# A decoder trunk of four layers: output products with tokens on partitions and 512 weight columns at a time, and layer boundaries taken in two halves of the tokens

## The chip, the cores and the metric

The kernel runs on one core of one Trainium2 chip. The metric is device microseconds of one execution. All inputs lie in HBM when it starts, and the output is written back there. The engines are TensorE (PE in the profile; PEld is its loading of weights), VectorE (DVE), ScalarE (ACT), GpSimd (POOL) and SyncE (SP), which issues the large DMAs.

## What is computed

A residual stream `h` of 256 tokens by 1024 channels passes four layers. Each layer has a token mixer and a gated feed-forward with a convolution of width 3 along the tokens; around each of them stand two RMS norms:

```python
for i in range(4):
    a = rms_norm(h, mix_norm_pre[i])
    m = mixer(i % 3)(a)          # 0: dilated attention, 1: short gated convolution, 2: conformer convolution
    h = h + rms_norm(m, mix_norm_post[i])
    f = conv_ffn(rms_norm(h, ffn_norm_pre[i]), ffn_w_in[i], ffn_w_conv[i], ffn_w_out[i])
    h = h + rms_norm(f, ffn_norm_post[i])

def conv_ffn(x, w_in, w_conv, w_out):
    u = causal_dwconv(x @ w_in, w_conv)      # w_in: 1024 x 5632
    g, v = split(u, 2)
    return (silu(g) * v) @ w_out             # w_out: 2816 x 1024
```

The layers are attention, short convolution, conformer, attention. Everything is float32. The attention has 16 heads of 64 in each of three groups with dilations 1, 4 and 16; its tokens are put in an order in which those with equal remainder by 4 lie together ("permuted"). The conformer's output product has a bias.

## The kernel before, in words

**Precision.** A float32 product is made of three products of `float32r` parts: weights and inputs are each split into a high part and a rest (`mm3`, L278). So each weight tile is copied by ScalarE (L192) and subtracted by VectorE (L198) before use.

**Weights.** `plan` (L68) lists all weights in order of use in pieces of 128 x 1024; two pieces make a block of 1 MB, which SyncE loads (L182) into one of three raw buffers. `Stream` hands the parts out: 11 slots for split pieces (`SLOTS`), and calls of `pump`, `copy`, `diff` and `between`, written by hand among the other work, split the pieces ahead. `take` gives the next piece, and splits it on the spot if that has not been done. The whole kernel runs under a manual schedule: each engine runs its instructions in the order in which they are written.

**Layout.** Channels lie on partitions, tokens in the free dimension. The residual is eight tiles `h[k]` of 128 channels x 256 tokens. A product uses a 128 x 128 weight tile as the stationary operand and 256 tokens as the moving one: `column` (L461) makes one tile of 128 output columns with 8 x 3 products of 256 columns. `Slabs` (L509) accumulates the second product of the feed-forward and of the short convolution row slab by row slab: one piece is 128 rows by 1024 columns, 24 products of 256 columns (L521) in four PSUM banks, issued between the columns of the first product as their inputs come (`ffn_steps`, `sc_steps`); the last rows go by column tiles (`tail`). In the attention four output columns are accumulated while the last head pairs are worked off (L1012 to L1022); the conformer's output goes by columns.

**The boundary.** `Out` (L469) squares each finished column tile on ScalarE and scales it by the norm's gain; the sums of squares go through `rstd_of` (L299): products with a column of ones (L305), then six small operations. `spread` (L319) brings the token scale to all channels, `warm` (L327) issues products of no use. `boundary` (L340) then scales, adds into the residual, and makes the two parts of the next input, channel tile by channel tile. `start_norm` and `ramp` (L424) run four column tiles of the next product at once as these parts come. The scale of the next norm is found meanwhile and multiplied in when the products are read out (`evac`, L573, and its like). The last `boundary` (L386 to L393) writes the output in four DMAs.

**PSUM.** Tag A has four banks, B three, S one. The work tiles `act` have 32 buffers of 128 x 512.

## Time and profile before

| | us |
|---|---|
| median of 3 runs | 1616.36 |
| lowest to highest | 1616.09 to 1616.82 |
| span of the profiled execution, first to last instruction | 1615.5 |
| busy: TensorE | 1589.8 |
| busy: VectorE | 1243.3 |
| busy: ScalarE | 924.9 |
| busy: GpSimd | 18.5 |
| DMA | 256.94 MB, mean 159 GB/s |

The page gives the profiled execution by its span; it gives no other time for it, and the median stands 0.9 us above. TensorE's matmuls are pipelined: a record's length is longer than the distance to the next record, and the pace is read from the starts. A float32 matmul that is not `float32r` leaves two records.

### The profile page before, as it was taken

How to read it: one execution, taken by the hardware profiler on the slowest of the kernel's cores; microseconds unless marked ns; L12 is line 12 of the kernel's file. 1: busy time of each engine (PE TensorE's matmuls, PEld its weight loads, DVE VectorE, ACT ScalarE, POOL GpSimd, SP SyncE). 2: the span in 40 equal slices, each digit the busy share in tenths (PEclk: the TensorE clock that was granted, in tenths of full speed). 3: DMA queues.
4: the chain of work that ended last, by engine and by line, in shares of the span. 5: the costliest groups of instructions: out<-in, count | busy, mean ns of one | idle time of the engine just before them, and what ended most of it. 6: DMA issues, size and time to landing. Idle time of an engine off the chain costs nothing.

```text
span 1615.5 us, 31426 instructions
## 1 busy us (share of the span) xinstructions
PE 1589.8 (98%) x13146; PEld 1554.8 (96%) x13146; DVE 1243.3 (77%) x2177; ACT 924.9 (57%) x1623; POOL 18.5 (1%) x51
## 2 busy tenths in 40 slices
PE   6999999999999999999999999999999999999998
PEld 6999999999999999999999999999999999999998
DVE  4987767697876779889599588785877778588783
ACT  6454644575564566556476666565645445566562
POOL 4000000000000000000000000000000000000000
PEclk9999999999999999999999999999999999999999
DMA  5553442265552644655243136553543434236540
GB/s 213 214 213 121 170 144 105 90 235 199 183 185 95 216 157 160 232 183 191 97 150 112 53 127 230 192 183 132 186 180 133 155 131 157 105 131 227 191 157 27
DMA packets 36718, 256.94 MB, mean 159 GB/s; under 512 B 4320, under 2 KB 4448, under 8 KB 5984
## 3 DMA queue, kind: packets, MB, share of 16 engines
q1 hardware_dynamic: 36288, 254.93, 44.0%
q8 instruction: 103, 1.69, 0.4%
q14 instruction: 39, 0.32, 0.1%
q10 hardware_dynamic: 288, 0.01, 0.0%
HBM read 253.87 MB, written 1.05 MB: 158 GB/s over the span
## 4 chain that ended last, share of the span: by engine, by line
PE 95%; DVE 2%; POOL 1%; ACT 1%; DMA 1%; issue 0%; DVEq 0%; POOLq 0%
PE psA L521 17%; PE psB L281 10%; PE psB L280 10%; PE psB L279 10%; PE psA L279 8%; PE psA L280 7%; PE psA L281 7%; PE psA L877 3%; PE psA L879 3%; PE psA L878 3%; PE psB L714 2%; PE psB L896 2%; PE psB L925 2%; PE psA L437 2%; PE psA L432 2%; PE psB L914 2%
## 5 line engine op out<-in xcount | busy, mean ns | idle before, releaser
L198 DVE TENSOR_TENSOR wlo<-raw,whi 128x1024 fp32r<-128x1024 f32 x480 | 579.9, 1220 | 41.8 <-ACT whi L192 40.6
L192 ACT CAST whi<-raw 128x1024 fp32r<-128x1024 f32 x480 | 490.0, 1046 | 22.2 <-DMA raw<-in_w_dram 16.6
L281 PE MATMUL psB<-act,wlo 128*128 128x256 f32 x1392 | 394.2, 283 | 0.0
L280 PE MATMUL psB<-act,whi 128*128 128x256 f32 x1392 | 394.2, 283 | 0.0
L279 PE MATMUL psB<-act,whi 128*128 128x256 f32 x1392 | 394.2, 283 | 0.0
L279 PE MATMUL psA<-act,whi 128*128 128x256 f32 x1040 | 303.6, 292 | 8.0 <-ACT whi L192 7.1
L281 PE MATMUL psA<-act,wlo 128*128 128x256 f32 x1040 | 295.2, 284 | 0.5 <-DVE wlo L198 0.5
L280 PE MATMUL psA<-act,whi 128*128 128x256 f32 x1040 | 295.3, 284 | 0.1
L521 PE MATMUL psA<-act,whi 128*128 128x256 f32 x1536 | 278.0, 283 | 0.0
L279 PEld LDWEIGHTS psB<-act,whi 128*128 128x128 f32 x1392 | 267.4, 192 | 0.0
L281 PEld LDWEIGHTS psB<-act,wlo 128*128 128x128 f32 x1392 | 267.4, 192 | 0.0
L280 PEld LDWEIGHTS psB<-act,whi 128*128 128x128 f32 x1392 | 267.4, 192 | 0.0
L521 PEld LDWEIGHTS psA<-act,whi 128*128 128x128 f32 x1536 | 239.7, 192 | 0.0
L521 PE MATMUL psA<-act,wlo 128*128 128x256 f32 x768 | 217.5, 283 | 0.0
L279 PEld LDWEIGHTS psA<-act,whi 128*128 128x128 f32 x1040 | 200.0, 192 | 12.8 <-ACT whi L192 7.1
L281 PEld LDWEIGHTS psA<-act,wlo 128*128 128x128 f32 x1040 | 200.1, 192 | 0.8 <-DVE wlo L198 0.8
L280 PEld LDWEIGHTS psA<-act,whi 128*128 128x128 f32 x1040 | 200.2, 192 | 0.6 <-DVE act L284 0.5
L290 ACT ACTIVATE tmp<-act,par 128x256 f32<-128x256 f32 x176 | 80.1, 502 | 176.6 <-DVE act L284 176.6
L287 DVE SCALAR_TENSOR_TENSOR tmp<-act,par,tmp 128x255 f32<-128x255 f32 (+1 forms) x352 | 146.6, 478 | 19.7 <-ACT tmp L290 19.7
L521 PEld LDWEIGHTS psA<-act,wlo 128*128 128x128 f32 x768 | 147.5, 192 | 0.0
L284 DVE TENSOR_TENSOR act<-psB,act 128x512 f32<-128x512 f32 (+2 forms) x94 | 58.4, 624 | 101.5 <-PE psB L281 60.1
L877 PE MATMUL psA<-whi,act 128*128 128x256 f32 x384 | 112.4, 293 | 0.0
(124 smaller groups left out, 2129.7 us busy)
## 6 DMA issues: line engine op xcount, KB each, us to landing
raw<-in_w_dram SPq DMA_DIRECT2D x239, 1024.0 KB, 4.8
h<-in_xT_dram SPq DMA_DIRECT2D x4, 256.0 KB, 5.1
raw<-in_w_dram SPq DMA_DIRECT2D x2, 512.0 KB, 5.5
out_dram<-h SPq DMA_DIRECT2D x4, 256.0 KB, 2.1
msk<-in_masks_dram SPq DMA_DIRECT2D x1, 512.0 KB, 9.4
par<-in_params_dram SPq DMA_DIRECT2D x1, 484.0 KB, 10.1
cst<-in_consts_dram SPq DMA_DIRECT2D x1, 132.0 KB, 5.9
par<-in_params_dram ACTq DMA_DIRECT2D x1, 4.0 KB, 2.9
```

The source lines that it names most:

```text
L192: self.nc.scalar.copy(out=hi, in_=raw)
L198: self.nc.vector.tensor_tensor(out=lo, in0=raw, in1=hi.bitcast(F32), op=ALU.subtract)
L279: nc.tensor.matmul(o, lhsT=whi, rhs=x[0], start=first, stop=False)
L280: nc.tensor.matmul(o, lhsT=whi, rhs=x[1], start=False, stop=False)
L281: nc.tensor.matmul(o, lhsT=wlo, rhs=x[0], start=False, stop=last)
L284: nc.vector.tensor_tensor(out=out, in0=a, in1=b, op=op)
L287: nc.vector.scalar_tensor_tensor(out=out, in0=a, scalar=s, in1=b, op0=op0, op1=op1)
L290: nc.scalar.activation(out=out, in_=a, func=AF.Identity, scale=s, bias=b)
L521: nc.tensor.matmul(o, lhsT=a, rhs=b, start=first and i == 0, stop=last and i == 2, skip_group_check=True)
L877: nc.tensor.matmul(oc, lhsT=xh, rhs=whi[:, k % 4, :], start=k == 0, stop=False)
L878: nc.tensor.matmul(oc, lhsT=xh, rhs=wlo[:, k % 4, :], start=False, stop=False)
L879: nc.tensor.matmul(oc, lhsT=xl, rhs=whi[:, k % 4, :], start=False, stop=k == KD - 1)
```

## The change

Output products turn round: 128 tokens of the input are the stationary operand and 512 weight columns the moving one (`Rows`), with all output pieces loaded as row slabs. The result has tokens on partitions, and so have the residual `h`, both norms and the output; gains come as rows spread over all partitions by a DMA on GpSimd's queue. `close` holds the last slabs (`HOLD`, 6; 5 in the short convolution), finishes the first half of the tokens (`product(0, e)`), then the second, and works off the norms of a half behind its products; transposes on TensorE turn the normed input back to channels (`turn`), and the parts go into one tile `xall`. The first four column tiles of the next product are made in the same form, a half at a time (`First`), and transposed; the second attention doesn't use `First`. Norm scales are no longer multiplied in at read-out. Slots go from 11 to 10, `act` buffers from 32 to 24, PSUM tags to four banks each.

```diff
-SLOTS = 11
-NACT = 32
+SLOTS = 10
+NACT = 24
+HOLD = 6
...
+    class First:
+        def product(self, c):
+            if self.ws is None:
+                self.ws = [st.take(HALF) for _ in range(4)]
+                st.held = 4
+            o = psum("A")
+            for k in range(KD):
+                whi, wlo, _ = self.ws[k // 2]
+                hi, lo = [chunk(a, c) for a in self.xs[k]]
+                w = k % 2
+                for i, (a, b) in enumerate(((hi, whi), (hi, wlo), (lo, whi))):
+                    nc.tensor.matmul(o, lhsT=a, rhs=b[:, w, :], start=k == 0 and i == 0, stop=k == KD - 1 and i == 2)
+                if c:
+                    st.held -= k % 2
+            z = act()[:].rearrange("p s t -> p (s t)")
+            nc.scalar.copy(out=z, in_=o)
+            self.zs[c] = z
+        def turn(self, c):
+            for i, o in enumerate(self.outs):
+                nc.tensor.transpose(chunk(o, c), self.zs[c][:, i * P:(i + 1) * P], ident)
...
+    class Rows:
+        def __init__(self, bias=None):
+            self.banks = [[banks[:, 2 * c + e, :] for e in range(2)] for c in range(2)]
+            turns["A"] = 0
+            self.begun = bias is not None
+            if self.begun:
+                for c in range(2):
+                    for e in range(2):
+                        nc.tensor.matmul(self.banks[c][e], lhsT=unit, rhs=bias[e],
+                                         start=True, stop=False)
+        def mm(self, c, e, w, x, last=False):
+            cs, es = slice(c * P, (c + 1) * P), slice(e * HALF, (e + 1) * HALF)
+            for i, (a, b) in enumerate(((x[0], w[0]), (x[0], w[1]), (x[1], w[0]))):
+                nc.tensor.matmul(self.banks[c][e], lhsT=a[:, cs], rhs=b[:, 0, es], start=not self.begun and i == 0,
+                                 stop=last and i == 2)
+        def add(self, x):
+            w = st.take(D)
+            for c in range(2):
+                for e in range(2):
+                    self.mm(c, e, w, x)
+            self.begun = True
+        def close(self, xs, post, pre, permuted=False):
             nc.scalar.preload_act_table(AF.Sqrt)
+            gpost = gain_tile(post, "gpost")
+            gpre = None if pre is None else gain_tile(pre, "gpre")
+            ws = [st.take(D) for _ in xs]
+            n = st.held = len(xs)
...
+            def squares(src):
+                s = tiny(1)
+                nc.scalar.activation(out=act()[:].rearrange("p s t -> p (s t)"), in_=src, func=AF.Square, accum_out=s)
+                return s
+            def product(c, e):
+                for i, (w, x) in enumerate(zip(ws, xs)):
+                    self.mm(c, e, w, x, i == n - 1)
...
+                o = self.banks[c][e]
+                s, m = squares(o), act()[:].rearrange("p s t -> p (s t)")
+                TT(m, o, gpost[:, e, :], ALU.mult)
+                return s, m
...
+            def follow(c, parts):
+                r = rstd(parts[0][0], parts[1][0])
+                ss, out_ = [], []
+                for e, (_, m) in enumerate(parts):
+                    STT(h[c][:, e, :], m, r, h[c][:, e, :], ALU.mult, ALU.add)
+                    if pre is None:
+                        nc.sync.dma_start(out=out[c * P:(c + 1) * P, e * HALF:(e + 1) * HALF], in_=h[c][:, e, :])
+                    else:
+                        ss.append(squares(h[c][:, e, :]))
...
+                r = rstd(*ss)
+                for e in range(2):
+                    x = act()[:].rearrange("p s t -> p (s t)")
+                    STT(x, h[c][:, e, :], r, gpre[:, e, :], ALU.mult, ALU.mult)
+                    out_.append(x)
+                return out_
+            def turn(c, x):
+                os = [psum("B") for _ in range(2)]
+                for e, o in enumerate(os):
+                    for i in range(4):
+                        nc.tensor.transpose(o[:, i * P:(i + 1) * P], x[e][:, i * P:(i + 1) * P], ident)
...
+                        src = o.rearrange("p (k t) -> p k t", k=4)
+                        hi, lo = [a[:, :, c * P:(c + 1) * P] for a in to]
+                        nc.scalar.copy(out=hi, in_=src)
+                        TT(lo, src, hi.bitcast(F32), ALU.subtract)
+            parts = []
+            for e in range(2):
+                st.pump(2, 0)
+                parts.append(product(0, e))
+            x0 = follow(0, parts)
+            parts = [product(1, e) for e in range(2)]
+            if x0:
+                turn(0, x0)
+            x1 = follow(1, parts)
+            def rest():
+                warm(4)
+                turn(1, x1)
+            return nxt, rest
+    def begin(xs, rest, outs):
+        f = First(xs, outs)
+        f.product(0)
+        rest()
+        st.pump(2)
+        f.product(1)
+        f.turn(0)
+        return lambda: f.turn(1)
...
         def evac(bank, f):
-            u = act()
-            TT(u, bank[:].rearrange("p (s t) -> p s t", s=2), bc2(rb), ALU.mult)
-            ts = taps3([u[:, e, :] for e in range(2)], f"fconv{l}_", (f, KF + f), between)
+            ts = taps3(halves(bank), f"fconv{l}_", (f, KF + f), between)
...
+        rows = Rows(bias)
+        for k in range(KD - HOLD):
+            rows.add(ys[k])
+            between()
+        return rows.close(ys[KD - HOLD:], 4 * l + 1, 4 * l + 2)
...
+            rest()
+            st.pump(2)
+            nc.scalar.preload_act_table(AF.Exp)
         first = [psum("A") for _ in range(2)]
+        for o in halves(first[0]) + halves(first[1]):
+            column(xs, o)
...
-        ws = [st.take() for _ in range(4)]
-        st.held = 4
-        os = [psum("A")[:, :T] for _ in range(4)]
-        for k in range(KD):
-            while work and (ys[k] is None or k < KD - 1):
+        rows = Rows()
+        for k in range(KD - HOLD):
+            while work and ys[k] is None:
                 step()
                 st.pump(1)
...
+            rows.add(ys[k])
+            step()
+            st.pump(1)
+        while work:
+            step()
+            st.pump(1)
+        return rows.close(ys[KD - HOLD:], 4 * l + 1, 4 * l + 2)
```

The diff is cut: the constructors, the permuted form of `turn` (eight slices of 128 instead of two of 512), the short convolution's and the conformer's use of `begin`, and the packing on the host follow the same pattern. `rstd` there has six operations of one column each.

## Rows read from the trace of the kernel before

**Rows 1.** The page, parts 1 and 4: busy time by engine; shares of the last chain.

```profile
PE 1589.8 (98%) x13146; PEld 1554.8 (96%) x13146; DVE 1243.3 (77%) x2177; ACT 924.9 (57%) x1623; POOL 18.5 (1%) x51
...
PE 95%; DVE 2%; POOL 1%; ACT 1%; DMA 1%; issue 0%; DVEq 0%; POOLq 0%
```

**Rows 2.** Windows: us, busy us of PE, PEld, DVE, ACT, POOL, clock, DMA share, GB/s.

```profile
312.00:495.00 183.00, 183.00 (x1528) 183.00 (x1527) 145.53 (x235) 109.39 (x173) 0.00 (x0) 1.00 0.54 190
```

**Rows 3.** The chain of waits in order of time: start us, us, what.

```profile
461.17 34.57 PE psA L521 x288
...
818.30 11.23 PE psB L714 x52
```

**Rows 4.** Timeline of TensorE, 30 to 36 us: start us, us, instruction.

```profile
31.96 0.41 PE L877 MATMUL psA<-whi,act 128*128 128x256 f32 x1
...
33.67 0.41 PE L879 MATMUL psA<-whi,act 128*128 128x256 f32 x1
```

**Rows 5.** Windows of 1 us (the clock stands behind POOL's column).

```profile
32.00:33.00 1.00, 1.00 (x6) 1.00 (x6) 0.00 (x0) 0.99 (x3) 0.00 (x0) 0.50 0.00 0
497.00:498.00 1.00, 0.83 (x5) 0.43 (x3) 0.53 (x5) 0.17 (x1) 0.00 (x0) 1.00 0.00 0
897.00:898.00 1.00, 1.00 (x6) 0.83 (x6) 0.40 (x4) 1.00 (x1) 0.00 (x0) 0.83 0.00 0
898.00:899.00 1.00, 1.00 (x6) 0.91 (x6) 0.23 (x1) 0.15 (x1) 0.00 (x0) 0.50 0.00 0
901.00:902.00 1.00, 1.00 (x10) 1.00 (x9) 0.66 (x2) 1.00 (x3) 0.00 (x0) 0.96 0.00 0
```

**Rows 6.** Timeline, 495 to 501 us: the boundary into the short convolution.

```profile
495.44 0.28 PE L521 MATMUL psA<-act,wlo 128*128 128x256 f32 x1
...
496.20 0.52 PEld L305 LDWEIGHTS psS<-cst,tmp 128*128 128x128 f32 x4 [0.22 <-ACT tmp L489]
...
496.84 0.17 DVE L308 RECIPROCAL tiny<-psS 128x2 f32<-128x2 f32 x1 [3.06 <-PE psS L305]
...
500.35 0.39 PE L437 MATMUL psA<-act,whi 128*128 128x256 f32 x1
```

**Rows 7.** Groups of instructions by line and shape, VectorE then ScalarE.

```profile
L284 DVE TENSOR_TENSOR act<-psA,act 128x512 f32<-128x512 f32 x64 | 43.3, 677 | 6.1 <-ACT act L335 6.1
...
L287 DVE SCALAR_TENSOR_TENSOR act<-h,par,act 128x256 fp32r<-128x256 f32 x64 | 31.5, 531 | 9.3 <-ACT act L290 9.3
...
L366 ACT ACTIVATE act<-h 128x512 f32<-128x512 f32 x24 | 14.2, 616 | 0.0
L905 ACT ACTIVATION_READ_ACCUMULATOR act<-act,tiny 128x1 f32 x64 | 11.9, 186 | 0.0
```

**Rows 8.** Timeline, 266 to 301 us, TensorE then VectorE: the first attention's tail.

```profile
267.88 1.96 PE L925 MATMUL psB<-act,act 128*64 128x256 f32 x24
...
281.94 0.60 PE L914 MATMUL psB<-cst,act 128*128 128x128 f32 x4
...
299.60 0.28 PE L281 MATMUL psB<-act,wlo 128*128 128x256 f32 x1
...
270.86 0.69 DVE L903 CUSTOM_DVE_ANT_0 act<-psB,msk 128x512 f32<-128x512 f32 x1 [0.15 <-PE psB L896]
...
273.05 0.68 DVE L903 CUSTOM_DVE_ANT_0 act<-psB,msk 128x512 f32<-128x512 f32 x1
```

**Rows 9.** Timeline of TensorE, 1119 to 1139 us: into the second attention.

```profile
1119.52 0.28 PE L521 MATMUL psA<-act,wlo 128*128 128x256 f32 x1
...
1124.68 0.39 PE L437 MATMUL psA<-act,whi 128*128 128x256 f32 x1 [0.24 <-ACT act L290]
```

**Rows 10.** Timeline, 1604 to 1616 us: the end.

```profile
1603.97 0.54 PEld L305 LDWEIGHTS psS<-cst,tmp 128*128 128x128 f32 x4
...
1612.11 0.33 SPq L393 DMA_DIRECT2D out_dram<-h  x1
```

**Rows 11.** Window of the first idle place of TensorE (columns as in rows 2).

```profile
25.00:30.00 5.00, 0.40 (x5) 0.31 (x3) 0.42 (x3) 0.24 (x3) 3.15 (x14) 0.73 0.12 51
```

More of the change, by code (lines that the diff above doesn't have):

```diff
@@ L70, in plan, with first, slab @@
     nt = 3 * NH * DH
+    def first(name, j, starts):
+        for k0 in range(0, KD, 2):
+            yield name, j, k0, 2, [(c, P) for c in starts]
+    def slab(name, j, s):
+        return name, j, s, 1, [(0, D)]
     for l in range(DEPTH):
@@ L110, in order @@
+        yield from first("ffn_w_in", l, [0, F, P, F + P])
+        for what, i in ffn_steps():
+            if what == "col" and i > 1:
+                for c in (0, F):
+                    yield "ffn_w_in", l, 0, KD, [(c + i * P, P)]
+            elif what == "slab":
+                yield slab("ffn_w_out", l, i)
 def order(quad):
@@ L114, in order, with steps @@
     return [(b[0], int(b[1])) for b in blocks.split()]
-FF_HEAD = KF - 8
-SC_HEAD = KD - 4
-def steps(n, head, held, start):
+def steps(n, hold, held, start):
     s = 0
@@ L126, in steps @@
         for _ in range(3):
-            if i >= start and s <= i - 3 and s < head - held:
+            if i >= start and s <= i - 3 and s < n - hold - held:
                 yield "slab", s
                 s += 1
-    while s < head:
+    while s < n - hold:
         yield "slab", s
         s += 1
-    for d in range(KD):
-        yield "tail", d
+    yield "close", None
+    while s < n:
+        yield "slab", s
+        s += 1
 def ffn_steps():
-    return steps(KF, FF_HEAD, 4, 6)
+    return steps(KF, HOLD, 4, 6)
 def sc_steps():
-    return steps(KD, SC_HEAD, 2, 5)
+    return steps(KD, 5, 2, 5)
 class Stream:
@@ L553, in taps3, with ffn @@
         return ts
-    def ffn(l, mg, rb):
-        xs, acc = boundary(mg, rb, f"fpre{l}")
+    def ffn(l, xs, rest):
         gs = []
@@ L582, in evac @@
                 gate()
-        banks = [psum("A") for _ in range(4)] + [psum("B") for _ in range(3)]
-        rb, scale = spread_later(start_norm(xs, acc, halves(banks[0]) + halves(banks[1])))
+        firsts = [banks[:, i, :] for i in (2, 3)]
+        turns["A"] = 0
+        second = begin(xs, rest, halves(firsts[0]) + halves(firsts[1]))
         nc.scalar.preload_act_table(AF.Silu)
-        slabs, out_ = Slabs(), None
+        rows = Rows()
         for what, i in ffn_steps():
@@ L646, in short_conv, with conformer @@
             elif what == "slab":
-                slabs.add(ys[k])
+                rows.add(ys[k])
                 between()
             else:
-                if out_ is None:
-                    out_ = Out(f"mpost{l}")
-                o = slabs.tail(k, ys[SC_HEAD:])
-                out_.evac(k, o)
-                if out_.n < 4:
-                    st.pump(1)
-        return out_.end()
-    def conformer(l, mg, rb):
-        xs, acc = boundary(mg, rb, f"mpre{l}")
+                break
+        return rows.close(ys[len(ys) - 5:], 4 * l + 1, 4 * l + 2)
+    def conformer(l, xs, rest):
         NP = KD // 2
-        banks = [[psum("A") for _ in range(2)] for _ in range(2)]
-        rb, scale = spread_later(start_norm(xs, acc, halves(banks[0][0]) + halves(banks[0][1])))
+        bk = [[banks[:, i, :] for i in (2, 3)], [banks[:, i, :] for i in (0, 1)]]
+        turns["A"] = 0
+        second = begin(xs, rest, halves(bk[0][0]) + halves(bk[0][1]))
+        turns["A"] = 0
         nc.scalar.preload_act_table(AF.Sigmoid)
```

489 lines of the change are left out of this document (187 added, 302 removed).

## The prediction

> **What bounds the kernel now.** I read the page first: TensorE is busy 98% of the span and carries 95% of the chain that ended last; VectorE has 77%, ScalarE less [rows 1]. One feed-forward stretch by windows says the same where the work is done: TensorE 183.0 of 183 us, VectorE 145.5, ScalarE 109.4 [rows 2]. So a change pays through the number and the pitch of TensorE's products and through the places where it waits; work taken from VectorE pays only there.
>
> The pitch comes from the chain of waits. 288 products of 256 columns take 34.57 us, 0.120 us each; 52 records of plain float32 with 256 columns take 11.23 us, 0.216 us each, every one with a weight load of its own [rows 3]. A stretch at half clock tells what the 0.120 is made of: from 31.96 to 33.67 there are eight steps of 0.214 us [rows 4] at a granted clock of 0.50 (window 32 to 33 [rows 5]), which is 256 columns at one per cycle of 1.2 GHz. At 2.4 GHz the same columns need 0.107 us, so something else sets 0.120. The weight loads do: four whose product has a single column follow each other in (0.52 - 0.19) / 3 = 0.11 us [rows 6]. A 256-column product is thus paced by its load; a 512-column one should be paced by its columns, 512 / 2.4 = 0.213 us or more.
>
> **The sum, part by part**, against the span of the profiled execution, 1615.5 us (the median of the runs is 0.9 us above it).
>
> *1. Wider products.* Each row slab of an output product has 24 products of 256 columns; it gets 12 of 512 (2 token halves, 2 column halves, 3 terms). Slabs: 22 in each of 4 feed-forwards, 8 in each of 4 mixers, 120, hence 1440 products. The first four column tiles of the next product (`First`) go the same way at six boundaries, 48 products each, 288; the second attention has none. The price of one lies between 0.213 us (columns alone) and 0.240 us (twice today's). I take 0.216 us, from the nearest row, the float32 record, which also streams 512 cycles over a load [rows 3]. Gain 1728 x 0.024 = 41.5 us; at the ends of the range 46.7 and 0.
>
> *2. Six ordinary boundaries* (attention to feed-forward twice, feed-forward to short convolution and to conformer, and both of these to feed-forward). Before: the last product starts at 495.44, the next layer's first at 500.35 [rows 6], 4.8 us beyond one pitch, filled with chain and warm-up products; four norm and four spreading products inside the next layer add 0.9 us (0.52 for such a four [rows 6], taken for both and rounded down). 5.7 us. After, counted from the end T0 of the last product of the second half:
> - The first half's chain hides under the second half's products, 36 x 0.216 = 7.8 us. It needs square with its accumulator read 0.62 + 0.19, norm 0.97 (six small operations of 0.16, as at 496.84 [rows 6]; the passes [rows 7]), two sums at 0.75 (an estimate: 0.53 at 256 columns plus about half of that for twice the columns; a two-operand pass of 512 takes 0.68), squares, norm, two scalings: 7.4 us. It just fits. The short convolution holds five slabs, 6.5 us: 1.0 exposed once.
> - At T0 eight transposes, 0.7 (the record of four, 0.60 [rows 8], less the 0.25 in which its last one overlaps what follows, twice); ScalarE first squares the second half, then casts 512 columns, VectorE takes the difference: the third product can start at 2.35, 1.9 us lost.
> - `First` for half 0, 24 products, runs to 7.1 and hides part of the second half's chain, which starts behind those differences at 2.95 and ends at 8.8. Four warm-up products (1.7 us) and eight transposes stand in TensorE's queue, then cast and difference again: half 1 starts at 10.2, 3.1 us lost.
> - Eight transposes back to channels, 0.7.
>
> Together 5.8 us against 5.7: the split hides about what the transposes and casts cost. Where the next layer begins thinner stocks show (10 weight slots for 11, six held to T0): 0.5 us at each feed-forward, as ScalarE must pass two columns' scalings and a SiLU, behind taps of some 0.5 each, before it copies piece seven; 0.6 at the short convolution, whose second transposes wait for their copy. In all +4.2 us.
>
> *3. Feed-forward to second attention.* No `First` covers there: `rest` runs at once. Before, first product 5.0 us after the last one's end [rows 9], stalls of 1.9 in its ramp and 0.5 for spreading, 7.4 in all. After, the second chain ends near 9.5 (the permuted parts go in slices of 128) and columns start at 10.2. +2.8 us. TensorE idles 6 us, so I let the clock fall, as it had at 32 us after the start's idle [rows 5]; the nearest rows with a price are those of the conformer's layer norm, 0.83, 0.50 three times (898 to 901) and 0.96 by windows of 1 us [rows 5], which lack 1.7 us in all. +4.5 us.
>
> *4. The end.* Before: from the last norm's start at 1603.97 to 1612.11, where the last output DMA is issued [rows 10], 8.1. After: square, norm and two sums for half a tile, 4 us, and the same 3.4 us of DMA. -4.0 us.
>
> *5. The tail of both attentions.* Now the last head pair's softmax runs beside four output columns, 12 products per input, and TensorE never stops. After, only two slabs (2.6 us each) are left to interleave; six are held. In the first layer's time: the pair before is weighted until 269.8 (267.88 + 1.9), then come slab, scores (0.95, from 269.8 to VectorE's first pass at 270.86), slab, scores. VectorE turns out one softened tile per 2.19 us (270.86 to 273.05 [rows 8]); begun at 273.4, four are ready at 282.2; transposes, copies and the weighted values (1.9) end at 285.25. Then 72 x 0.216 = 15.6 us of products are left: 300.8, where now the last starts at 299.60 [rows 8]. With the 2.3 us that this layer had under part 1, 3.4 us. TensorE does under 2 us of work in 6.5, so again 1.7 for the clock. Two layers: +10.2 us.
>
> *6. The conformer's bias* becomes four float32 products of 512 columns before the first slab: two records each, at twice 0.216, 3.4 us, in a place where TensorE follows on directly. +3.4 us. Nothing, if they slip under the wait for the first input.
>
> *7. Start and loads.* 1 MB more of x and gain rows on POOL's queue, 7.7 MB over the run. The first idle place takes 4.6 of 5 us with DMA at 0.12 [rows 11]; that cover gone, 1 MB would cost 5.3 us at the 190 GB/s of [rows 2]. I take 0.5. The gain tiles are wanted a layer after their buffers come free: nothing, covered by that layer.
>
> *8. The clock at the six boundaries.* What TensorE does there was not seen: two stretches of 1.7 to 2.4 us with transposes and idling. The old boundary kept 1.00 (497 to 498); in the layer norm it fell, after some 2 us of single-column products. Each fall costs 1.7 us. Between 0 and 12 falls, 0 and 20 us; I take three, the longer stretches at half the boundaries, 5.0 us.
>
> VectorE loses 0.69 us per feed-forward column pair (88 of them) and that is worth nothing: it was not the bound.
>
> Sum: -41.5 + 4.2 + 4.5 - 4.0 + 10.2 + 3.4 + 0.5 + 5.0 = -17.7. Span 1597.8, median about 1598.5 us.
>
> **Rivals.**
> - *Clock and chains at every boundary.* If the clock falls in all twelve stretches (15 us more than taken) and each chain is 0.5 us longer, 1616: no change. For it: the fall in the layer norm. Against: dense products stand between the stretches. Chance 0.10 (half of it within 0.2%).
> - *A 512-column product costs two of 256.* If the 0.120 came with the columns, part 1 vanishes and the costs stay: 1598.5 + 41.5 = 1640, slower. It decides from 0.226 us upward (1728 x 0.0138 us uses up the costs of 23.8). Against: 0.214 at half clock, where an overhead per column would show too. Chance 0.05.
> - *Boundaries better covered.* No falls at boundaries, bias hidden: 1590. Chance 0.20.
> - *Columns past 256 nearly free.* If a product stayed at its load's 0.12 us whatever its width, 1728 x 0.096 more: 1433. The 0.214 at half clock and the 0.216 record say that columns are paid one by one. Chance 0.01. The Trainium skill (TensorE: Matmul & The Clock Gate, Back-to-back issue gap) speaks for something like it: in a stream of loads and products, 131 ns at 512 columns; by it part 1 would be an estimated 188 us and the time 1452, and no row here agrees with it.
>
> **How the numbers follow.** The forecast as summed has 0.64. 0.2% of the time, 3.2 us, is what a measurement can tell from no change. The range goes from 1583 (no falls anywhere, which is 10 us, and the bias and the price of 0.214 for the rest) to 1618 (every stretch falls), which leaves out the two last rivals and a part of the unforeseen. Faster 0.86, same 0.06, slower 0.08 (the doubled price, and part of the first rival).
>
> **What would show it.** Pitch of the slab products in the chain: 0.216 right, 0.24 wrong. Between the last slab product and the dense run of the next layer: two gaps of about 2 and 3 us. The granted clock in windows of 1 us at each boundary. A gap of about 5 us in each attention's tail, ending on ScalarE's copies of transposed weights; 10 us before the second attention. Feed-forwards of 183 instead of 191 us. I am wrong if the slabs don't run dense, or if new waits on weight parts (the 10 slots) show in TensorE's waits.

## The result, and the profile after

The changed kernel took 1631.1 us (median of 4 runs) against 1616.4 of the kernel before: ratio 1.0095, 95% interval 1.0080 to 1.0109. The forecast was 1598.5 us and faster; the time is 13 us above its range. The profiled execution of after has a span of 1633.7 us (before 1615.5); it is the longest of the four (1635.5 us, the others 1630.4 to 1631.3), so what is read from its trace adds up to more than the 14.7 us between the medians.

The page of after, parts 1 and 4 (to set beside [rows 1]):

```profile
PE 1562.3 (96%) x11394; PEld 1446.6 (89%) x11394; DVE 1176.5 (72%) x2052; ACT 891.5 (55%) x1587; POOL 27.1 (2%) x68
...
PE 89%; DVE 5%; ACT 2%; DMA 1%; POOL 1%; issue 1%; DVEq 0%; ACTq 0%; POOLq 0%
```

TensorE is busy 27.5 us less than before, as the change wants, yet the span is 18 us longer: in the chain that ended last TensorE's share has fallen by 6 points, and VectorE's has risen by 3. What TensorE waited for, by line (waits of after: us in total, times, longest):

```profile
PE banks L440 <- DVE wlo L209: 17.4, 5, 3.6
PE banks L536 <- DVE act L309: 10.4, 2, 8.3
PE banks L934 <- DVE act L928: 8.5, 5, 2.7
...
PE banks L301 <- DVE act L306: 5.4, 1, 5.4
```

L440 are the products of `First`, L536 the transposes between two layers, L934 those of the softened tiles. The first line has a boundary to itself. Timeline of after at the end of the first attention, TensorE and then VectorE (start us, us, instruction):

```profile
312.61 1.03 PE L536 MATMUL banks<-cst,act 128*128 128x128 f32 x8
314.02 0.50 PE L440 MATMUL banks<-whi,xall 128*128 128x512 f32 x1 [0.38 <-ACT xall L548]
...
322.66 0.80 PE L440 MATMUL banks<-wlo,xall 128*128 128x512 f32 x1 [3.61 <-DVE wlo L209]
...
324.96 2.39 PE L352 MATMUL banks<-cst 128*128 128x256 f32 x8
327.18 1.04 PE L536 MATMUL banks<-cst,act 128*128 128x128 f32 x8
328.46 0.50 PE L440 MATMUL banks<-whi,xall 128*128 128x512 f32 x1 [0.24 <-ACT xall L548]
...
320.06 1.42 DVE L309 SCALAR_TENSOR_TENSOR act<-h,tiny,gpre 128x512 f32<-128x512 f32 x2
321.39 1.22 DVE L209 TENSOR_TENSOR wlo<-raw,whi 128x1024 fp32r<-128x1024 f32 x1
```

`First`'s first half stops after 19 of its 24 products. It wants the low part of the fourth weight piece, and that difference (321.39) stands in VectorE's queue behind the whole norm chain of the second half (its last step is at 320.06). The half that was to hide the chain so waits for its end, and the second half starts 15.9 us after the last slab product (312.61 to 328.46) where 10.2 were forecast. The clock goes too, by windows of after (columns as in [rows 2]; the granted clock stands behind POOL's):

```profile
318.50:323.50 5.00, 1.39 (x5) 0.86 (x4) 3.47 (x8) 0.37 (x3) 0.53 (x1) 0.90 0.10 30
323.50:328.40 4.90, 4.72 (x20) 3.72 (x19) 0.00 (x0) 1.17 (x3) 0.00 (x0) 0.75 0.87 294
```

The pitch, which is the distance from the start of one product to the start of the next: in the chain of after, against the 34.57 us of [rows 3] for 288 products, which are 144 of the new width,

```profile
480.07 27.22 PE banks L468 x120
```

and of the timeline the first product of two columns and the first product behind them:

```profile
406.84 0.28 PE L301 MATMUL banks<-xall,whi 128*128 128x256 f32 x1
...
412.50 0.39 PE L468 MATMUL banks<-whi,act 128*128 128x512 f32 x1
```

A slab product of 512 columns takes 27.22 / 120 = 0.2268 us, not 0.216. And 48 column products, which the change leaves 256 wide, take 5.66 / 48 = 0.1179 instead of 0.1200; over all of them (6548 intervals between starts) the mean is 0.1164.

By stages of the two timelines, each ended by its last slab product: first attention +12.9 us, its feed-forward -1.2, short convolution and feed-forward -0.8, conformer +8.0, feed-forward -3.2, second attention +7.2, last feed-forward -0.2, end -4.5; together the 18.2 us of the spans.

### The profile page after: what moved, and what is told of

It reads as the page before. It is cut to its first block, busy times and chain, and to the rows that moved or that the text cites. A ratio compares the mean times of both kernels' runs of the same rounds, so it can differ in the third digit from the quotient of the medians.

```text
span 1633.7 us, 27744 instructions
## 1 busy us (share of the span) xinstructions
PE 1562.3 (96%) x11394; PEld 1446.6 (89%) x11394; DVE 1176.5 (72%) x2052; ACT 891.5 (55%) x1587; POOL 27.1 (2%) x68
## 4 chain that ended last, share of the span: by engine, by line
PE 89%; DVE 5%; ACT 2%; DMA 1%; POOL 1%; issue 1%; DVEq 0%; ACTq 0%; POOLq 0%
PE banks L468 19%; PE banks L301 16%; PE banks L302 16%; PE banks L303 16%; PE banks L440 3%; PE banks L894 3%; PE banks L732 3%; PE banks L896 3%; PE banks L895 3%; PE banks L945 2%; PE banks L916 2%; PE banks L934 2%; DVE wlo L209 1%; PE banks L352 1%; ACT act L490 1%
## 5 line engine op out<-in xcount | busy, mean ns | idle before, releaser
L301 PE MATMUL banks<-xall,whi 128*128 128x256 f32 x2304 | 654.3, 284 | 12.1 <-ACT whi L203 6.8
L303 PE MATMUL banks<-xall,wlo 128*128 128x256 f32 x2304 | 646.4, 281 | 0.5 <-DVE wlo L209 0.5
L302 PE MATMUL banks<-xall,whi 128*128 128x256 f32 x2304 | 646.2, 280 | 0.0
L209 DVE TENSOR_TENSOR wlo<-raw,whi 128x1024 fp32r<-128x1024 f32 x480 | 576.1, 1221 | 57.9 <-ACT whi L203 56.3
L301 PEld LDWEIGHTS banks<-xall,whi 128*128 128x128 f32 x2304 | 437.0, 190 | 17.6 <-ACT whi L203 12.3
L303 PEld LDWEIGHTS banks<-xall,wlo 128*128 128x128 f32 x2304 | 440.0, 191 | 1.1 <-DVE wlo L209 1.0
L302 PEld LDWEIGHTS banks<-xall,whi 128*128 128x128 f32 x2304 | 436.0, 189 | 1.5
L468 PE MATMUL banks<-whi,act 128*128 128x512 f32 x960 | 306.4, 392 | 0.0
L309 DVE SCALAR_TENSOR_TENSOR tmp<-banks,par,tmp 128x255 f32<-128x255 f32 (+1 forms) x352 | 145.3, 475 | 144.4 <-ACT tmp L312 144.4
L468 PEld LDWEIGHTS banks<-whi,act 128*128 128x128 f32 x960 | 181.5, 189 | 38.8 <-ACT act L789 1.5
L468 PE MATMUL banks<-wlo,act 128*128 128x512 f32 x480 | 187.8, 391 | 0.0
L894 PE MATMUL banks<-whi,xall 128*128 128x256 f32 x384 | 112.0, 292 | 3.0 <-ACT whi L203 3.0
L925 ACT ACTIVATE act<-act,tiny 128x512 f32<-128x512 f32 x64 | 46.4, 725 | 116.9 <-DVE tiny L923 116.9
L896 PE MATMUL banks<-whi,xall 128*128 128x256 f32 x384 | 108.8, 283 | 0.0
L894 PEld LDWEIGHTS banks<-whi,xall 128*128 128x128 f32 x384 | 74.0, 193 | 4.8 <-ACT whi L203 3.1
L896 PEld LDWEIGHTS banks<-whi,xall 128*128 128x128 f32 x384 | 74.0, 193 | 0.0
```

The lines of the kernel that those rows point to most:

```text
L209: self.nc.vector.tensor_tensor(out=lo, in0=raw, in1=hi.bitcast(F32), op=ALU.subtract)
L301: nc.tensor.matmul(o, lhsT=whi, rhs=x[0], start=first, stop=False)
L302: nc.tensor.matmul(o, lhsT=whi, rhs=x[1], start=False, stop=False)
L303: nc.tensor.matmul(o, lhsT=wlo, rhs=x[0], start=False, stop=last)
L309: nc.vector.scalar_tensor_tensor(out=out, in0=a, scalar=s, in1=b, op0=op0, op1=op1)
L468: nc.tensor.matmul(self.banks[c][e], lhsT=a[:, cs], rhs=b[:, 0, es], start=not self.begun and i == 0, stop=last and i == 2)
```

## The experiments

Times are medians; the kernel before took 1616.2 to 1616.8 us beside them.

**1. The stuck difference.** One line in `close`, after the second `st.pump(2, 0)`:

```diff
             for e in range(2):
                 st.pump(2, 0)
+                if e:
+                    st.diff()
                 parts.append(product(0, e))
```

> The changed kernel with one line more: in the close of a slab stage, the difference of the fourth weight piece is given to VectorE before the second half's norm chain instead of behind it. Theory 'stuck difference': of the wait in the first products (17.4 + 5 + 3.6 us seen on L440 for L209) nearly all goes, and the half clock and part of warm(4) behind it: 5 boundaries by about 5 us, so 25 to 30 us less than the changed kernel, about 1603 us (ratio to the kernel before 0.990 to 0.994), and First's second half starts about 10 us after the last slab product where it now starts 16. Rival 'the norm chain itself is the boundary': turn(1) waits for the chain anyway, the wait only moves from the first products to the fill, 0 to 5 us less, about 1628 us (ratio 1.006 to 1.009).

1608.1 us, ratio 0.9953 (0.9939 to 0.9967): 23.0 us less than the changed kernel. The wait on L209 in `First` is gone from the list of waits. The theory holds, a little smaller than its figure.

**2. Ten slots in the kernel before.** `SLOTS = 11` becomes 10.

> The kernel before with ten slots of weights in place of eleven, nothing else. Theory 'the slot costs the start': the copies of weight pieces come one piece later and queue behind ScalarE's readings of the values; the end of attention 0's first weighing comes 9 to 12 us later than 91.9 us, and the whole takes 9 to 12 us more, about 1627 us (ratio 1.006 to 1.008). Rival 'the extra transfers at the start (the second copy of x and the gains)', which this kernel does not have: the first weighing within 2 us of 91.9 us and the whole within 2 us (ratio 0.999 to 1.001).

1621.8 us, ratio 1.0030 (1.0018 to 1.0042). The slot costs 5.6 us there, but not at the start: the first weighing of values (L925), by which the start is timed here, is at 91.6 us (91.9 before). Both theories missed. Of the 5.6 us, 2.0 are waits on differences (L281 for L198: 2.5 us in 6, before 0.5 in 1); the rest was not traced.

**3. Eleven slots in the changed kernel.** `SLOTS = 11`, and `NACT` 24 becomes 20 to make room.

> The changed kernel with eleven slots of weights again and 20 activation buffers in place of 24. Theory 'the slot costs the start': 9 to 11 us less than the changed kernel, the first weighing at about 93 us instead of 103.4 (about 1621 us, ratio 1.002 to 1.004). Rival 'the extra transfers': first weighing at 101 us or later, 0 to 2 us less (ratio 1.008 to 1.0095).

1606.7 us, ratio 0.9939 (0.9926 to 0.9951): 24.4 us less, and the first weighing still at 102.5 (103.4 with ten). So the start is not the slots' doing, and what the slot does cost is the boundary, as its timeline there shows:

```profile
313.82 1.03 PE L536 MATMUL banks<-cst,act 128*128 128x128 f32 x8
315.24 0.50 PE L440 MATMUL banks<-whi,xall 128*128 128x512 f32 x1 [0.38 <-ACT xall L548]
...
321.25 1.89 PE L352 MATMUL banks<-cst 128*128 128x256 f32 x8
...
324.25 0.50 PE L440 MATMUL banks<-whi,xall 128*128 128x512 f32 x1 [0.24 <-ACT xall L548]
```

No stop, and the second half starts 10.4 us after the slabs. This is run 1 by another way: six held slabs and four pieces of `First` are ten, so with ten slots the fourth piece is the last one copied, and `pump` leaves the newest copy's difference for later, here for `take` inside `First`, which is emitted after the chain. An eleventh slot lets a fifth copy in, and the fourth difference goes out ahead of the chain. The boundary behind the short convolution is the counterpart: it holds five slabs, so nine pieces, and it is the one boundary with `First` that has no wait of L440 on L209 with ten slots. Runs 1 and 3 take away the same wait, 17.4 us in all, so their gains should not be added; the two edits were not run together.

The start has its own rows in the same kernel (TensorE, then VectorE):

```profile
44.56 0.36 PE L894 MATMUL banks<-whi,xall 128*128 128x256 f32 x1 [2.96 <-DVE act L306]
...
57.34 0.55 PE L301 MATMUL banks<-xall,whi 128*128 128x256 f32 x1 [5.36 <-DVE act L306]
...
43.74 0.67 DVE L306 TENSOR_TENSOR act<-banks,act 128x512 f32<-128x512 f32 x1
...
56.52 0.67 DVE L306 TENSOR_TENSOR act<-banks,act 128x512 f32<-128x512 f32 x1
```

Both waits end on a rotation of queries and keys that reads a PSUM bank. The change deals the four A banks of PSUM in a fixed turn; the kernel before took from a pool of four. The second values' turn falls on the bank of the first queries, whose rotation VectorE has not reached.

**4. Banks by release.** On run 3's kernel, in attention:

```diff
+        free = [(turns["A"] + i) % 4 for i in range(4)]
+        def bank():
+            n = free.pop(0)
+            return n, banks[:, n, :]
...
-            o = psum("A")
+            n, o = bank()
...
+                free.append(n)
```

(`append` stands where the bank's last reader has been issued. The edit is cut: `bank` also serves the queries and keys.)

> The changed kernel with eleven slots and 20 activation buffers (the kernel of the run before), and in attention the four A banks of PSUM are handed out in the order in which their readers were issued, as the pool of the kernel before did, in place of the fixed turn. Theory 'the fixed turn costs the start': in attention 0 the second values take the bank that the first values have just left and not the one whose rotation VectorE has yet to read; the waits of 2.96 us (L894 for L306) and 5.36 us (L301 for L306) go, and the half clock behind them: the first weighing at about 92 us in place of 102.5, the whole 10 to 12 us less, about 1596 us (ratio 0.987 to 0.988). Rival 'the extra transfers at the start (second copy of x, gains)': the waits move to a transfer, first weighing at 100 us or later, 0 to 2 us less (ratio 0.9925 to 0.994).

1593.8 us, ratio 0.9860 (0.9846 to 0.9873): 12.9 us less; both waits (8.3 us) are gone, the first weighing is at 89.5 us, and the granted clock from 40 to 60 us is 1.00 in each window of 5 us. The extra transfers cost nothing that shows.

**5. The width alone, undone.** On run 3's kernel, in `Rows.mm` (1380 of 1440 products):

```diff
-                nc.tensor.matmul(self.banks[c][e], lhsT=a[:, cs], rhs=b[:, 0, es], ...)
+                start, stop = not self.begun and i == 0, last and i == 2
+                for s in range(1 if start or stop else 2):
+                    n = HALF if start or stop else T
+                    nc.tensor.matmul(self.banks[c][e][:, s * n:(s + 1) * n], lhsT=a[:, cs],
+                                     rhs=b[:, 0, e * HALF + s * n:e * HALF + (s + 1) * n], ...)
```

> Width alone undone, on the changed kernel with eleven slots (1606.7 us): 1380 of the 1440 slab products of 512 columns are given as two of 256, everything else stays. Theory 'one fixed step per product' (pitch 0.0145 us and 0.4167 ns a column, read from the width lines): two halves cost 0.0145 to 0.0148 us more than the whole, 1380 times is 20 us more, about 1627 us (ratio 1.006 to 1.0075). Rival 'the forecast's step of 0.024 us' (0.120 twice against 0.216): 33 us more, about 1640 us (ratio 1.0145). A third way, width is not on the path that ends: under 5 us more.

1610.2 us, ratio 0.9966 (0.9954 to 0.9977): only 3.5 us more. The chain of this kernel in the stretch of slabs (the 120 products stand as 236 records: 116 in two halves, four left whole), and its timeline over two columns:

```profile
476.43 28.76 PE banks L471 x236
```

and

```profile
404.88 0.29 PE L301 MATMUL banks<-xall,whi 128*128 128x256 f32 x1
...
410.34 0.39 PE L471 MATMUL banks<-whi,act 128*128 128x256 f32 x2
```

The slabs did slow down, to 0.120 us a half, which is some 18 us (1380 x 0.0132). But the columns, untouched, fell to 5.46 / 48 = 0.1138 here and to 0.1144 in the mean (0.1161 in run 3), and gave 6912 x 0.0017 = 12 us back. The third way has the right number, under 5 us, but not the ground: the width is on the path, and another gain hid it. No theory had that gain: the pitch of a product is not a matter of its width alone.

**6. The pitch by itself.** The layer is left out: TensorE alone, in lines of 36 products.

> No layer at all: the computation is left out, TensorE alone runs lines of 36 products from fixed buffers, one width and form per line, so the output is not the layer's. Disputed is what sets 0.2268 us for a 512-column product. Theory 'a fixed part per product': pitch of single-pass products rises in a straight line with the columns and a step of about 0.010 to 0.014 us in front (128 columns 0.065, 256 columns 0.118, 384 columns 0.172, 512 columns 0.226), and the plain float32 record of 256 columns, which is two passes, is 0.216 as in the slabs of before. Rival 'the weight load of 512-column products is not hidden': 512 columns with the same weights each time, or with 64-column weights, comes down to 0.216 us, with new weights stays at 0.227. Rival 'the banks': 512 columns into four banks in turn differ from 512 into one by 0.005 us or more.

Timeline; a line's pitch is the distance to the next start over its products:

```profile
25.75 4.13 PE L254 MATMUL banks<-xa,wa 128*128 128x128 f32 x36
29.72 4.53 PE L256 MATMUL banks<-xa,wa 128*128 128x256 f32 x36
34.09 6.43 PE L258 MATMUL banks<-xa,wa 128*128 128x384 f32 x36
40.36 8.36 PE L260 MATMUL banks<-xa,wa 128*128 128x512 f32 x36
48.56 8.32 PE L262 MATMUL banks<-xa,wa 128*128 128x512 f32 x36
56.72 8.44 PE L264 MATMUL banks<-xa,wa 128*64 128x512 f32 x36
65.00 4.25 PE L266 MATMUL banks<-xa,wa 128*64 128x256 f32 x36
69.09 8.35 PE L268 MATMUL banks<-xa,wa 128*128 128x512 f32 x36
77.28 15.70 PE L270 MATMUL banks<-raw 128*128 128x256 f32 x72
92.63 4.66 PE L272 MATMUL banks<-xa,wa 128*128 128x256 f32 x36
```

256, 384 and 512 columns: 0.1214, 0.1742, 0.2278, a straight line of columns at 2.4 GHz plus 0.0145 (at 256 the first interval is a long one; without it the line has 0.1200). 128 columns stand at 0.110, no lower than the four loads of [rows 6] (0.11). At 512 columns the same weights each time (L262: 0.2267), half as many weight columns (L264: 0.230) or four banks (L268: 0.2275) change little. At 256 columns half as many weight columns do change something: 0.1136 (L266). So a load has a part in the pitch of the narrow product, though the step stands at the wide ones too. The float32 record hardly has such a step: its 72 starts lie 0.2158 apart, (15.70 - 0.38) / 71, and each float32 product is two records. So the nearest row that the forecast took, 0.216, was of another kind of product.

**7. What moves it.** TensorE alone again, lines of 96 products in a column's order.

> No layer again: the computation is left out, TensorE runs lines of 96 products of 256 columns from fixed buffers in the order of a column (high weights by high and low input, low weights by high input). Disputed is why the same columns run at 0.1200 us in the kernel before, at 0.1178 or 0.1135 in the changed one, and on average faster when the slabs are halved. Theory 'addresses': the lines with weights or input moved by 8 or 16 floats differ from the unmoved ones by 0.004 us or more, the unmoved ones agree with each other. Theory 'a phase set by what ran before': unmoved lines differ among each other, after one odd product of 128 or 512 columns. Theory 'traffic of the other engines': the line beside ScalarE's copies or VectorE's differences is slower by 0.004 us or more than the others.

```profile
45.96 11.68 PE L267 MATMUL banks<-xa,wa 128*128 128x256 f32 x96
57.48 11.52 PE L269 MATMUL banks<-xa,wa 128*128 128x256 f32 x96
68.84 11.47 PE L271 MATMUL banks<-xa,wa 128*128 128x256 f32 x96
80.15 11.48 PE L273 MATMUL banks<-xa,wa 128*128 128x256 f32 x96
91.46 11.47 PE L275 MATMUL banks<-xa,wa 128*128 128x256 f32 x96
...
125.81 11.68 PE L284 MATMUL banks<-xa,wa 128*128 128x256 f32 x96
137.33 11.68 PE L289 MATMUL banks<-xa,wa 128*128 128x256 f32 x96
```

Every unmoved line takes 0.1200 us (at most 0.1204), also after an odd product (L267) and beside copies and differences of the other engines (L284, L289). With the weights moved by 8 floats it is 0.1183 (L269), by 16 floats 0.1178 (L271), with the input moved by 8 or by 16 floats 0.1178 (L273, L275). Moving an address does it, at half the size that was expected; that the lines before have no say is shown for unmoved operands alone.

**8. By offset.** TensorE alone, the moving operand shifted against the stationary one.

> No layer: lines of 96 products, nine with 256 and nine with 512 columns, the moving operand 0, 4, 8, 16, 24, 32, 64, 128 and 240 floats off the place at which it is congruent to the stationary one. Theory 'one collision at equal addresses': 256 columns 0.1200 us at 0 and 0.1178 to 0.1183 at each other offset; 512 columns 0.2268 at 0 and 0.2245 elsewhere. Theory 'each offset has its own step': some offsets stand at 0.1135, and 512 columns follow the same order. Rival 'addresses do not matter to 512 columns': 0.2265 to 0.2270 on all nine lines.

Floats of offset 0, 4, 8, 16, 24 for 256 columns (L265 to L273), 0, 4, 8, 16 for 512 (L283 to L289):

```profile
22.39 11.68 PE L265 MATMUL banks<-xa,wa 128*128 128x256 f32 x96
33.91 11.56 PE L267 MATMUL banks<-xa,wa 128*128 128x256 f32 x96
45.31 11.36 PE L269 MATMUL banks<-xa,wa 128*128 128x256 f32 x96
56.52 11.04 PE L271 MATMUL banks<-xa,wa 128*128 128x256 f32 x96
67.39 11.68 PE L273 MATMUL banks<-xa,wa 128*128 128x256 f32 x96
...
124.23 21.94 PE L283 MATMUL banks<-xa,wa 128*128 128x512 f32 x96
146.01 22.40 PE L285 MATMUL banks<-xa,wa 128*128 128x512 f32 x96
168.24 22.57 PE L287 MATMUL banks<-xa,wa 128*128 128x512 f32 x96
190.65 22.14 PE L289 MATMUL banks<-xa,wa 128*128 128x512 f32 x96
```

256 columns: 0.1200, 0.1188, 0.1168, 0.1132, 0.1200; also 0.1186 at 32 floats, 0.1200 at 64 and 128, 0.1135 at 240. 512 columns: 0.2269, 0.2316, 0.2334, 0.2289; 0.2268 at 64 and 128, 0.2333 at 32 and 240. The step differs from offset to offset, and the two widths order the offsets differently. But the offset does not settle it alone. Run 7 had its operands at the same addresses, and there the input moved by 8 and by 16 floats took 0.1178 both times, where it takes 0.1168 and 0.1132 here. The lines before and the PSUM bank differ between the two runs; which of them matters was not tested. Two halves at 16 floats cost as much here as one whole at 0 (2 x 0.1132 against 0.2269).

In the kernel before, the inputs stand at the same address as the weights modulo 1024 bytes. In the changed one a new tile, `xall`, holds the columns' inputs, and it happens to stand 64 bytes below, by two small tiles (`epsd`, `pi`) allocated between it and the weights. Two kernels test what that does.

**9. The kernel before, activations moved.**

```diff
+    pad = ap.tile([P, 240], F32, tag="pad", name="pad", bufs=1)
+    nc.vector.memset(pad, 0.0)
     par = cp.tile([P, NPAR], F32, name="par")
```

> The kernel before with one empty tile of 960 bytes ahead of the activations, so that their addresses stand 64 bytes off those of the weights (modulo 1024), as the inputs of the columns do in the changed kernel; nothing else. Theory 'addresses' (the moved lines of 256 columns took 0.1178 and 0.1183 us, the unmoved 0.1200): the 10752 products of 256 columns of this kernel fall to between 0.1135 and 0.1183 us, which is 18 to 70 us, of which the boundaries and the other engines leave most: about 1575 to 1598 us (ratio 0.974 to 0.989). Rival 'the pitch of 0.1200 belongs to the PSUM pools, or to the program of this kernel': no change, ratio 0.999 to 1.001.

1583.2 us, ratio 0.9772 (0.9748 to 0.9797), with nothing else touched. Its five runs spread from 1573.2 to 1584.1 us, wider than those of the kernel before; why, no kept trace shows. The same stage as in [rows 3], in its chain:

```profile
451.67 33.94 PE psA L523 x288
```

0.1178 us for 0.1200 in the slabs, 0.1167 in the mean of the columns.

**10. The changed kernel, inputs moved back.** On run 12's kernel (1585.2 us):

```diff
+    pads = [cp.tile([P, 16], F32, name="pad0")]
     xall = cp.tile([P, KD, 2, T], F32R, name="xall")
+    pads.append(cp.tile([P, 240], F32, name="pad1"))
+    for t in pads:
+        nc.vector.memset(t, 0.0)
```

> The kernel with the last pair's scores first (1585.2 us) and 64 empty bytes ahead of the tile of inputs, 960 behind it, so that the inputs of the columns stand at the same address modulo 1024 as the weights; all else is at its old distance. Theory 'the columns' gain is the address': the columns go back to 0.1200 us, 6912 times 0.0037 is 25 us more, about 1610 us (ratio 0.995 to 0.998). Rival 'it is the PSUM tile or another part of the change': within 3 us of 1585 us (ratio 0.979 to 0.983).

1617.2 us, ratio 0.9996 (0.9988 to 1.0005): 32 us more. The columns are back at 0.1199 in the mean (0.1163 in run 12's kernel), the values at 0.1200 (0.1170): 6912 x 0.0036 + 1152 x 0.0030 = 28 us. The clock can hold the other 4: in the profiled execution its mean is 0.989 (0.993 in run 12's kernel), with 0.50 for 3.4 us in each attention's tail, where run 12's kernel has 1.00; and of the eleven runs those at 0.991 to 0.994 took 1612.9 to 1615.1 us, those at 0.989 1617.2 to 1618.7.

**11. The bias early.** On run 4's kernel, the bias and `Rows(bias)` move up to replace `warm(6)` in the layer norm.

> The kernel of the banks by release, and in the conformer the bias products are issued where six warming products stood, in the layer norm, so that their transfer and their 4.4 us (L462 x8) lie in time in which TensorE waits for the norm. Theory 'the bias lies on the path': 4 to 6 us less than the kernel of the banks by release. Rival 'it lies in a wait that the norm of the layer makes anyway, the end of the slabs is set by VectorE's last outputs': within 1.5 us of it.

1591.7 us, ratio 0.9847 (0.9834 to 0.9861): 2.1 us less, between the two theories, with overlapping intervals.

**12. The last scores first.** On run 4's kernel, three `step()` ahead of the two slabs of the attention's tail, two after each.

> The kernel of the banks by release, and at the end of both attentions the scores of the last pair are issued ahead of the two slab outputs that now stand before them. Theory 'the two slabs hold up the chain of the last softening': it begins 2.8 us sooner, TensorE's waits for L928 (9.0 us in 6) shrink by 5 to 7 us, the whole by 5 to 8 us against the kernel of the banks by release. Rival 'the chain of VectorE and ScalarE (four softenings of 2.6 us) has the length of the tail whatever stands ahead': the waits stay within 2 us, the whole within 2 us.

1585.2 us, ratio 0.9809 (0.9796 to 0.9823): 8.6 us less, and the waits on the softened tiles shrink from 8.7 us in run 4 to

```profile
PE banks L943 <- DVE act L937: 1.2, 2, 0.6
```

Of these 7.5 us, 4 come back on other lines of the tail (L954 now waits 3.5 us for ScalarE, L925 0.6 more). The clock gives the rest: in run 4's kernel it stands at 0.50 from 277.0 to 283.8 and from 1372.7 to 1379.5 us, with 10.7 us of work for TensorE, which is some 5 us lost; in this kernel it is 1.00 in both tails.

**13. Combinations.** Runs 4, 11 and 12 together, with 36 and then 18 products of warming in place of four before the second attention; and the latter with the inputs 64 bytes above the weights, by pads of 32 and 224 floats.

> Eleven slots, banks by release, the bias products early, the last pair's scores ahead of the two slabs, and 36 warming products in place of four at the boundary into the second attention (8.3 us of waiting on L536, then half clock). Theory: the parts add up: 1585.2 less 2.1 for the bias less 2 to 3 for the clock at that boundary, about 1581 us (ratio 0.977 to 0.9795). Rival 'a part gives back what another gained, or the warming products delay the transposes': 1584 us or more (ratio 0.980 or more).

> The kernel with all mended, with 18 warming products for 36 at the boundary into the second attention (each is two records of 0.216 us; 36 took 15.7 us and the transposes came at 1111.4, 6 us late). Theory: 7.8 us less than 1590.5, about 1582.7 us (ratio 0.977 to 0.980). Rival 'the warming is not what was lost': 1588 us or more (ratio 0.982 or more).

> The same kernel with 128 empty bytes ahead of the tile of inputs and 896 behind it, so that the inputs stand 64 bytes above the weights (modulo 1024) and not 64 below. Theory 'the offset sets the step': the columns, now a mix of 0.1135 and 0.1178, all go to 0.1132 as in the line of 16 floats, 6912 times 0.0030 is 21 us less than the 18-warm kernel, about 1562 us (ratio 0.965 to 0.969). Rival 'the mix comes of something else than the offset': the same mix, within 4 us of the 18-warm kernel.

1590.5 (ratio 0.9838, 0.9825 to 0.9852), 1585.2 (0.9803, 0.9790 to 0.9816) and 1594.6 us (0.9861, 0.9846 to 0.9876). The first theory fell on its size: a warming product is two records, so the filler took 15.7 us where the wait was 8.3. With 18 it fits, but bias and filler together bring nothing over run 12. The third fell as well: the mean of the columns is 0.1177 where 0.1163 was the mix, and 6912 x 0.0014 = 9.7 us is about what was lost (9.4). Moving the inputs changes the pitch in the whole kernel too, but not by the figures of TensorE alone.

## Why the prediction was wrong

Two steps failed outright, and they cost 37.3 us where the prediction had 2.6 us in all (0.5 at each feed-forward, 0.6 at the short convolution) and nothing.

- **Part 2, the thinner stocks** ("10 weight slots for 11, six held to T0"). The place, the start of the next layer, was right; the wait and its price were not: I looked at when a piece is copied, not at where its difference lands in VectorE's queue. The fourth piece's difference went behind the norm chain, and `First` waited for it at five boundaries. Measured by run 3: 24.4 us. With eleven slots the timing of part 2 is right at the first attention's boundary: the second half starts 10.4 us after the slabs (10.2 forecast). My last sentence named "new waits on weight parts (the 10 slots)" as what would make me wrong, and gave it no chance and no price.
- **Part 7, the start.** I priced the transfers and not the banks. The pool became a tile dealt in turns; the diff shows it, the prediction does not mention it. Measured by run 4: 12.9 us.

With both mended the kernel takes 1593.8 us, 4.7 under the forecast. That is partly luck, for **part 1** is wrong too, in its price and in its ground. A 512-column product was to cost 0.216; it costs 0.2268, so the slabs gained 1440 x 0.0132 = 19 us and `First`, at 0.229, 3 more, not 41.5. The ground was that a 256-column product is paced by its weight load, and a wide one by its columns alone. The step of about 0.0145 over the columns stands at 256, 384 and 512 columns alike (run 6), and the same loads run at 0.1132 in another place (run 8). A load has some part in it at 256 columns (L266 of run 6); how much, and what makes up the rest of the step, is open. Against the smaller gain stands one of which I expected nothing: the columns and values gained 6912 x 0.0036 + 1152 x 0.003 = 28 us by the address of a new tile, as run 10 shows. That makes 50 us of gains for 41.5, and with the two steps mended the other costs are 50 - 22.6 = 27 us, where the sum's other terms make 24. Undoing the width cost 3.5 us (run 5), since the columns of that kernel ran still faster.

The rest, by its terms:
- Part 3, second attention: the transposes waited 8.3 us in one piece where I had TensorE idle 6, and 5.6 us of work ran at half clock behind them, 2.8 us lost where 1.7 stood. Right in kind, too small.
- Part 4, the end: -4.5 (forecast -4.0).
- Part 5, the attentions' tails: in the first layer 34.9 us from the end of the last weighing but one to the last slab product, before 29.9. The 96 slab products in it gained 1.3 us under part 1, so the tail itself lost 6.3 us, where 5.1 were forecast.
- Part 6, the bias: L462 takes 4.4 us (3.4 forecast), the last part of it at a clock of 0.50. Issuing it earlier brought 2.1 us in run 11, with overlapping intervals, and nothing beside run 12's edit.
- Part 8, the clock: three falls were forecast at the six boundaries. With ten slots there are five (0.50 from 322.5, 517.1, 609.3, 810.6 and 1442.1 us on). With eleven there is none. Run 3's window over the first four, from the boundary behind the first attention to the one into the conformer (the other two lie in stretches of 1.00 as well):

```profile
297.40:898.20 600.80, 597.61 (x3991) 546.57 (x3990) 453.07 (x802) 354.59 (x637) 6.24 (x18) 1.00 0.49 172
```

The range has a slip of its own: every stretch falling adds 15 us to 1598.5, which is 1614 and not 1618, and the terms named for the lower end give 1582 and not 1583. The result lies above either.

Of the rivals, "clock and chains at every boundary" has the place and not the mechanism: the chain is as long as forecast (the second half's scaling ends 8.9 us after the slabs, forecast 8.8), and what is late is a weight piece. The doubled price named its tipping point at 0.226, and 0.2268 came; yet that is not what made the kernel slower, since the products as a whole gained more than forecast. "Boundaries better covered" came true in one half with eleven slots (no falls) and not in the other (the bias). "Columns past 256 nearly free" is excluded: no 512-column line is under 0.2267. The 131 ns that the Trainium skill (TensorE: Matmul & The Clock Gate, Back-to-back issue gap) gives does not hold for these products.

## What to carry to other kernels

When a change takes away a buffer, follow each queue to the step that used the last one: here a difference that no longer had a slot ahead of it went behind a 9 us chain, and cost 24 us. A fixed turn of banks is not a pool; write down who still reads the bank when its turn comes. Before pricing a wider product, try other addresses for the operands: here 960 empty bytes brought the old kernel 33 us, as much as the best version of the change (31).

## What the runs showed of the hardware

Not expected: the pitch of back-to-back `float32r` products changes when the stationary or the moving operand is moved in SBUF. At 256 columns it is 0.1200 us at equal addresses modulo 1024 bytes (runs 7 and 8), and between 0.1132 and 0.1178 at 64 bytes' distance; at 512 columns 0.2269 against 0.2289, with 0.2334 at 32 bytes. It needs no other engine's traffic (runs 7 and 8). The Trainium skill (SBUF — State Buffer, A bandwidth-pool intuition that's wrong (but worth ruling out)) gives the weight load a read port of its own, independent of the moving operand's; a pitch that changes with the distance of the two operands does not fit two reads that never touch each other.

At 64 bytes' distance there are two levels, and a stretch keeps the one that it begins with. In run 12's kernel the columns run in 121 uninterrupted stretches of 20 intervals or more: 2566 intervals lie in stretches with a mean of 0.1133 to 0.1143, 4048 in stretches of 0.1176 to 0.1178, and no stretch is in between. When only the slabs' form changes (run 5), the columns between the slabs go from 0.1178 to 0.1137 throughout. So what runs ahead of a stretch has a say in its level, and the same may lie behind the two figures for one address in runs 7 and 8.

Open: what picks the level. That the two reads collide in a bank is a guess; no run looked at it.
